# Opening in a hand-written order with squares summed on TensorE; hyperbolic tangents, split exponents and a filter emitted between the blocks

## The chip, the core and the metric

The kernel runs on one core of one Trainium2 chip. It is one launch that computes a whole inference step of a small four-stage network. The metric is the device time of the launch in microseconds (us), as the median of a few runs. The core has a matrix engine (PE, with its weight loads shown apart as PEld), a vector engine (DVE), a scalar engine with look-up functions (ACT), a general engine (POOL) and a queue processor that starts transfers (SP). Each engine works through its own list of instructions strictly in order and waits where the next one's inputs or buffers are not ready.

## The reference

Two groups of tokens, 128 context tokens and 512 latent tokens, run through one even and one odd layer at a width of 1024. The change touches only the first layer. Its first steps are an RMS norm over the width, an adaptive scale and shift made from the condition vectors, and one wide input projection:

```python
y = xf * lax.rsqrt(jnp.mean(xf * xf, axis=-1, keepdims=True) + EPS)    # norm, per token
h = y * (1 + scale) + shift             # scale, shift = linear map of silu(c)
proj = h @ P['ev_in_w'][e]
cv = _short_conv(proj[..., :EV_CONV], ...)
mq = jax.nn.silu(cv[..., o0:o0 + M_W])                 # mLSTM queries
mk = jax.nn.silu(cv[..., o0 + M_W:o0 + 2 * M_W])       # mLSTM keys
h = jax.nn.sigmoid(o) * h                              # mLSTM output gate
```

Beside the projection the kernel evaluates the long-convolution filter of the layer: a small network with sines on the positions (`_hyena_spectra`: features, sin, sin, a last linear map, an exponential window), normalised by the sum of magnitudes and transformed with a Fourier matrix. The mLSTM part then works in chunks, forwards and backwards, with exponents that are differences of running sums and maxima:

```python
dlog = jnp.where(mask, b[:, :, None] - b[:, None, :] + ic[:, None, :], -jnp.inf)
mt = jnp.maximum(b + m[:, None], jnp.max(dlog, axis=2))
w = jnp.exp(dlog - mt[:, :, None])          # weights within a chunk
a_in = jnp.exp(inter - mt)                  # weight of the state that comes in
```

## The kernel before, in words

Tokens (640 of them, 128 and 512) lie along the columns of a tile, the width along the partitions, so that x is eight tiles `x[0..7]` of 128x640. A matrix product that has to keep 32-bit accuracy is made of one-pass products of rounded operands: a tile is split into a high part (`hH`, `whi`, a rounding copy on ACT, L463 for weights and L1632 for activations) and a low part (`hL`, `wlo`, a subtraction on DVE or POOL, L464 and L1633). One step of a product is six matmuls, L1676 to L1681: high by high, low by high, high by low, each on 384 and on 256 columns. Eight such steps make an output tile of 128x640, called a block here. Data that is left as plain 32-bit floats goes through PE in slower matmuls, which the profile shows as two instructions each.

The first layer has these stages, in the order of the program.

- **Opening.** `mod_0` computes scale and shift (weights from `mod0`, 16 loads of 512 KB, matmuls at L1465, transposes at L1448). `norm_0` squares the eight x tiles on ACT (L1611), adds them up on DVE and POOL (seven additions, L1613, those in `RA` on POOL), lets PE sum over the partitions (five matmuls, L1551), takes the root on DVE (L1598 to L1603), spreads the result over the partitions (L1571 on DVE, L1575 on PE, L1580 on ACT), and multiplies x by it (L1619, the tiles in `XP` on POOL). Each tile is then scaled and shifted (L1629, L1631), rounded (L1632) and its low part is formed (L1633, those in `LP` on POOL). `sines` makes the inner network of the filter for three thirds of the positions (L509, L514, range reduction on DVE at L471 to L477). Only PE's order is written by hand here, by the string `START`, one letter for each step of the three generators (`m` modulation, `s` sines, `r` norm) and `g` for the first weights. The second eight loads of `mod0` each wait for a copy on POOL (L1440).
- **Blocks.** `mlstm_in` makes the gates' tile and the first convolution's tile (the two opening blocks), then seven more convolution blocks, the values (`values`, L807 to L810) and four gate blocks. `conv` (L639 to L648) is a three-tap convolution; the keys and queries go through Silu (L786, L787), the output gates through Sigmoid (L792) and a multiplication (L793). `mlstm_gates` does the running sums and maxima on DVE (L819 to L884).
- **Filter.** `filter` is emitted as a whole before `mlstm_in`: for two filters and two halves, three windows each (`windowed`, an exponential on ACT at L595, a product L602, magnitudes L604 and L606, sums L607, L610 and L611), a sum of magnitudes (`hy_norm`: L617 on DVE, L619 on PE, L622), and Fourier products (L557 to L559, L576 to L578).
- **mLSTM and the rest of the projection.** `mlstm` transposes the keys (L927), weights them (L940 on POOL), forms the states (L948 on PE, L950 and L952 on DVE) and then works through five chunks; its exponents come from 32-bit float matmuls (L990 and, for chunks 1 to 4, L1000) on right-hand sides that POOL and DVE prepare (`RH` at L979, L980 and L983). `hyena_in` makes the remaining blocks of the projection beside it.

Except for `START`, nothing sets the engines' orders by hand: the whole program runs under a list scheduler that simulates the engines while it takes the instructions in the order of emission, and it may put an instruction into another engine's idle time. A block's weights are loaded through a ring of tiles (`wraw`, four) and split into two pairs (`whi`, `wlo`). ACT holds one group of look-up functions at a time; changing the group costs an instruction of its own (ACT_TABLE_LOAD), and the list scheduler leaves them where the functions alternate.

## Time and profile before

| | us |
|---|---|
| median of 3 runs (2131.42 to 2133.31) | 2132.94 |
| the profiled execution | 2131.59 |
| its span | 2129.8 |
| PE busy in the span | 2005.5 (94%) |
| DVE busy | 1607.7 (75%) |
| ACT busy | 1099.9 (52%) |
| POOL busy | 740.3 (35%) |

The profiled execution took 1.79 us more than its span, and lies 1.35 us under the median. Times of the trace are counted from the start of the span. "Busy" of PE is the time with a matmul in flight; PE's clock is shown as the granted share of full speed, and everything that the change touches lies in the first 395 us, a fifth of the span.

### The profile page before, as it was taken

The page shows a single profiled execution, that of the slowest core. Times are in us where ns is not written, and L with a number is a line of the kernel's source. Part 1 is how long each engine was busy: PE and PEld are TensorE (multiplying, and loading weights), DVE is VectorE, ACT ScalarE, POOL GpSimd, SP SyncE. Part 2 cuts the span into 40 slices and gives each one's busy share as a digit, 9 for nine tenths or more (in the row PEclk, how much of TensorE's full clock was granted, in tenths as well). Part 3 has the DMA queues.
Part 4 walks back from the last instruction along what each step waited for, and adds up shares of the span by engine and source line. Part 5 has one row for each costly group of instructions (what it writes and reads, how often), then busy time and mean ns, then how long its engine had stood idle before and what let it go on. Part 6 is the DMA issues. An engine that isn't in the chain of part 4 may idle for free.

```text
span 2129.8 us, 35924 instructions
## 1 busy us (share of the span) xinstructions
PE 2005.5 (94%) x14034; PEld 1906.7 (90%) x14034; DVE 1607.7 (75%) x2685; ACT 1099.9 (52%) x1908; POOL 740.3 (35%) x751
## 2 busy tenths in 40 slices
PE   4999899998899999999899999999999899999997
PEld 2889788987899999999899899999999899999997
DVE  7875566787988888887687777776743988888885
ACT  3847634422655555555375556555522555555553
POOL 4411121343444443524232323333322343444422
PEclk9999999999899999999999999999999899999998
DMA  7654422764122222233222222121445122222221
GB/s 289 223 171 147 135 74 69 270 213 166 40 87 72 90 70 89 75 98 124 74 61 60 65 65 66 60 65 60 149 159 177 31 92 77 87 78 84 73 96 50
DMA packets 85637, 225.38 MB, mean 106 GB/s; under 512 B 9979, under 2 KB 27899, under 8 KB 85468
## 3 DMA queue, kind: packets, MB, share of 16 engines
q1 hardware_dynamic: 71756, 205.44, 29.4%
q10 hardware_dynamic: 8960, 9.86, 1.5%
q0 software_dynamic: 4752, 7.79, 1.4%
q8 instruction: 110, 1.80, 0.3%
q14 instruction: 59, 0.48, 0.1%
HBM read 204.86 MB, written 18.36 MB: 105 GB/s over the span
## 4 chain that ended last, share of the span: by engine, by line
PE 66%; DVE 14%; issue 2%; ACT 2%; DMA 2%; POOL 1%; SPq 0%; DVEq 0%; ACTq 0%; POOLq 0%
PE aux L2046 14%; PE mm L2046 14%; PE mm L1676 5%; PE mm L1680 5%; PE mm L1678 5%; PE mm L1677 3%; PE mm L1681 2%; PE mm L1679 2%; DVE x L1980 2%; PE aux L1321 1%; PE aux L1363 1%; PE aux L1342 1%; DVE sw L2012 1%; DVE wlof L2026 1%; PE md L1309 1%
## 5 line engine op out<-in xcount | busy, mean ns | idle before, releaser
L1680 PE MATMUL mm<-hH,wlo 128*128 128x384 f32 x760 | 264.0, 348 | 2.5 <-DVE wlo L464 2.5
L1676 PE MATMUL mm<-hH,whi 128*128 128x384 f32 x760 | 265.2, 349 | 1.2 <-ACT hH L1632 1.2
L1678 PE MATMUL mm<-hL,whi 128*128 128x384 f32 x760 | 263.5, 347 | 0.1
L463 ACT ACTIVATE whi<-wraw 128x1024 fp32r<-128x1024 f32 x108 | 114.1, 1056 | 205.7 <-PE mm L1679 109.3
L1677 PE MATMUL mm<-hH,whi 128*128 128x258 f32 (+1 forms) x568 | 168.9, 297 | 7.6 <-DVE U L641 7.4
L1679 PE MATMUL mm<-hL,whi 128*128 128x258 f32 (+1 forms) x568 | 167.3, 295 | 0.0
L1681 PE MATMUL mm<-hH,wlo 128*128 128x258 f32 (+1 forms) x568 | 166.5, 293 | 0.0
L464 DVE TENSOR_TENSOR wlo<-wraw,whi 128x1024 fp32r<-128x1024 f32 x94 | 120.6, 1283 | 46.5 <-ACT whi L463 42.2
L1680 PEld LDWEIGHTS mm<-hH,wlo 128*128 128x128 f32 x760 | 144.3, 190 | 6.5 <-issue 2.8
L1676 PEld LDWEIGHTS mm<-hH,whi 128*128 128x128 f32 x760 | 144.6, 190 | 4.8 <-issue 2.3
L1678 PEld LDWEIGHTS mm<-hL,whi 128*128 128x128 f32 x760 | 144.5, 190 | 2.6 <-issue 1.6
L464 POOL TENSOR_TENSOR wloe<-wraw,whie 128x512 fp32r<-128x512 f32 (+1 forms) x68 | 82.2, 1209 | 171.4 <-ACT whie L463 167.6
L1677 PEld LDWEIGHTS mm<-hH,whi 128*128 128x128 f32 x568 | 109.7, 193 | 12.4 <-issue 10.9
L1679 PEld LDWEIGHTS mm<-hL,whi 128*128 128x128 f32 x568 | 109.7, 193 | 2.3 <-issue 1.5
L1681 PEld LDWEIGHTS mm<-hH,wlo 128*128 128x128 f32 x568 | 109.7, 193 | 1.2 <-issue 0.5
L2026 DVE TENSOR_TENSOR wg<-sw,wg 128x1024 fp32r<-128x1024 f32 (+1 forms) x68 | 76.8, 1129 | 24.4 <-ACT wg L2007 23.4
L2007 ACT ACTIVATE wg<-sw 128x1024 fp32r<-128x1024 f32 (+1 forms) x68 | 64.4, 947 | 58.5 <-DVE sw L2016 37.6
L1318 POOL TENSOR_TENSOR xw<-xB,ec 128x256 f32<-128x256 f32 x64 | 49.2, 772 | 125.6 <-PE aux L1321 77.6
L2026 DVE TENSOR_TENSOR wlo<-wraw,whi 128x1024 fp32r<-128x1024 f32 (+1 forms) x68 | 76.7, 1128 | 15.5 <-ACT whi L2007 15.5
L2007 ACT ACTIVATE whif<-sw 128x1024 fp32r<-128x1024 f32 (+1 forms) x68 | 64.5, 948 | 39.7 <-DVE sw L2016 34.5
L2026 DVE TENSOR_TENSOR wlof<-sw,whif 128x1024 fp32r<-128x1024 f32 (+1 forms) x68 | 76.5, 1125 | 5.9 <-ACT whif L2007 5.2
L2166 ACT ACTIVATE nt<-nt 128x128 f32<-128x128 f32 x44 | 17.8, 404 | 109.5 <-POOL nt L2151 106.8
(804 smaller groups left out, 7160.2 us busy)
## 6 DMA issues: line engine op xcount, KB each, us to landing
wraw<-in_w SPq DMA_DIRECT2D x96, 512.0 KB, 3.5
modr<-in_modw SPq DMA_DIRECT2D x80, 512.0 KB, 6.1
wraw<-in_odw SPq DMA_DIRECT2D x49, 512.0 KB, 3.6
wraw<-in_w2q SPq DMA_DIRECT2D x48, 384.0 KB, 3.1
wraw<-in_evw SPq DMA_DIRECT2D x25, 512.0 KB, 4.2
wraw<-in_odow SPq DMA_DIRECT2D x16, 512.0 KB, 3.5
kd<-kst ACTq DMA_DIRECT2D x16, 256.0 KB, 2.6
wraw<-in_evow SPq DMA_DIRECT2D x8, 512.0 KB, 6.9
```

The source lines that it names most:

```text
L463: self.nc.scalar.activation(h, src, AF.Copy)
L464: (eng or self.nc.vector).tensor_tensor(lo, src, h.bitcast(F32), op=ALU.subtract)
L1318: nc.gpsimd.tensor_tensor(xw, xB[c][:, 0:256].rearrange("p (h e) -> p h e", h=4), self.ec[:, c, hd[d]].unsqueeze(2).to_broadcast([128, 4, ...
L1676: nc.tensor.matmul(pA, h, rh[k][:, 0:384], start=f, stop=False)
L1677: nc.tensor.matmul(pB, h, rh[k][:, 384:T_], start=f, stop=False)
L1678: nc.tensor.matmul(pA, h, rl[k][:, 0:384], start=False, stop=False)
L1679: nc.tensor.matmul(pB, h, rl[k][:, 384:T_], start=False, stop=False)
L1680: nc.tensor.matmul(pA, lo, rh[k][:, 0:384], start=False, stop=l)
L1681: nc.tensor.matmul(pB, lo, rh[k][:, 384:T_], start=False, stop=l)
L2007: vec, sub, copy = nc.vector.tensor_tensor, ALU.subtract, lambda o, v: nc.scalar.activation(o, v, AF.Copy)
L2026: vec(lo, r1 if step == "LA" else self.v, h.bitcast(F32), op=sub)
L2046: self.k.nc.tensor.matmul(bank, w, x, start=first and k == j == 0, stop=k == self.K - 1 and j == 2, skip_group_check=not first)
```

## The change

1. `start` takes the place of `mod_0` and `norm_0`, and the order of all engines is written by hand up to the end of the first two output tiles, not only PE's. The squares are still taken on ACT, but each square tile goes to PE directly: five matmuls a tile with the square as the weights and a column of ones as the moving operand, all 40 adding into one column group. All products of x with the root and all low parts of the activations are on DVE. The sines step one third after the other (`sine_steps`). The second eight loads of `mod0` no longer wait for copies on POOL. The two opening blocks are made in the order steps 0 to 3 of the first, shift and scale matmuls, steps 0 to 3 of the second, then steps 4 to 7 of both.
2. The filter is a generator that is advanced once after each convolution block, each gate block and every second value tile, and finished after `mlstm_in`.
3. Silu becomes a hyperbolic tangent and a DVE operation, y(1 + tanh y) on halved convolution weights; Sigmoid becomes a tangent of half the argument and (1 + tanh) times a halved factor.
4. The mLSTM exponents are made by one one-pass matmul each (18 of them) whose operands carry high and low parts in separate partitions. `mlstm` prepares the left sides once (`UR`) and the right sides' rows (`MR`, `XR`); each of the 18 then takes one DVE product of 128x512 (L997 of the new file).
5. Loads that waited for the last modulation matrix or for nothing (`filter_loads`, `mlc`) wait for the last low tile of the activations.

The core of the diff (long parts are left out where a line holds only three dots):

```diff
-START = 'sssmmrmmmrmmmmmrgsssmmmmmmmmmmr'
...
-                    with tc.manual_schedule(engines={mybir.EngineType.PE}):
-                        for c in START:
...
+                    with tc.manual_schedule():
+                        get, pr, pk, h2 = self.start(vp, fp, a, b, sq)
+                    self.filter_loads(fp, self.hL[LM].bitcast(F32)[:, 0:1])
                     self.load_mats(matp, self.hL[LM].bitcast(F32)[:, 0:1])
-                    f = self.filter(fp, h2)
-                    for _ in f:
-                        pass
+                    self.filt = self.filter(fp, h2)
                     self.bg.append(self.mod(0, (2, 3, 4, 5), fp, 4, self.mu[:, 0:1]))
...
-                    self.mlstm_in(vp, get)
+                    self.mlstm_in(vp, get, pr, pk)
                     self.mid = False
+                    for _ in self.filt:
+                        pass
...
-            nc.scalar.activation(o[:, 0:128], y[:, 0:128], AF.Silu)
-            nc.scalar.activation(o[:, 128:640], y[:, 129:641], AF.Silu)
+            for s, e, q in ((0, 128, 0), (128, 640, 1)):
+                nc.scalar.activation(o[:, s:e], y[:, s + q:e + q], AF.Tanh)
+                nc.vector.scalar_tensor_tensor(o[:, s:e], o[:, s:e], 1.0, y[:, s + q:e + q],
+                                               op0=ALU.add, op1=ALU.mult)
+            next(self.filt, None)
...
-                nc.scalar.activation(y[:, s:e], pr[g], AF.Sigmoid)
-            nc.vector.tensor_scalar(y[:, 0:T], y[:, 0:T], self.mng[:, h:h + 1], None, op0=ALU.mult)
+                nc.scalar.activation(y[:, s:e], pr[g], AF.Tanh, scale=0.5)
+            nc.vector.tensor_scalar(y[:, 0:T], y[:, 0:T], 1.0, self.mng[:, h:h + 1], op0=ALU.add, op1=ALU.mult)
...
+        fr = self.t(p, (128, T), "xm")
+        nc.vector.tensor_tensor(fr[64:128].rearrange("p (c s) -> p c s", s=128),
+                                MN[64:128].rearrange("p (c s) -> p c s", s=128),
+                                MP[64:128].unsqueeze(2).to_broadcast([64, 5, 128]), op=ALU.add)
+        UR, MR, XR = [], [], []
+        for d in range(2):
...
+            nc.scalar.activation(t, UL[d], AF.Copy)
+            nc.vector.tensor_tensor(t[other], UL[d][own], t[own].bitcast(F32), op=ALU.subtract)
+            nc.vector.tensor_copy(t[other2], UL[d][own2])
+            UR.append(t)
+            for src, lst, one in ((MN, MR, 1.0), (fr, XR, 0.0)):
+                t = self.t(p, (128, T), f"MX{d}{int(one)}", 1, F32R)
+                nc.gpsimd.memset(t[0:64].bitcast(F32), one)
+                nc.scalar.activation(t[own2], src[own2], AF.Copy)
+                nc.vector.tensor_tensor(t[other2], src[own2], t[own2].bitcast(F32), op=ALU.subtract)
+                lst.append(t)
...
-            nc.gpsimd.tensor_copy(RH[0:64], dl[0:64])
-            nc.vector.tensor_tensor(RH[64:128], mn, dl[64:128], op=ALU.mult)
-            if c:
-                RH2 = self.t(p, (128, 4, 128), "RH2", 2)[64:128]
-                stt(RH2, mn, MP[64:128, c:c + 1], dl[64:128], op0=ALU.add, op1=ALU.mult)
+            def exponents(src, d):
+                t = self.t(p, (128, 4, 128), "RH", 3, F32R)
+                nc.vector.tensor_tensor(t, src[d].bitcast(F32)[:, cs].unsqueeze(1).to_broadcast([128, 4, 128]), dl,
+                                        op=ALU.mult)
+                g = self.ps("aux")
+                nc.tensor.matmul(g, UR[d][:, cs], t.rearrange("p h t -> p (h t)"), start=True, stop=src is XR)
+                return g
...
+        def square(d):
             nc.scalar.activation(sq[d], self.x[d], AF.Square)
-        for i, (a, b) in enumerate(((0, 1), (2, 3), (4, 5), (0, 2), (6, 7), (4, 6), (0, 4))):
-            (nc.gpsimd if i in RA else nc.vector).tensor_tensor(sq[a], sq[a], sq[b], op=ALU.add)
+            for c in range(5):
+                nc.tensor.matmul(pc[:, c:c + 1], sq[d][:, 128 * c:128 * c + 128], self.ones[:, 0:1],
+                                 start=False, stop=d == 7 and c == 4)
...
+        product(0, range(4))
+        mods(1, 1, range(4))
+        ev = evac(1)
+        step(0)
+        turn(1, 1, ev)
+        product(1, range(4))
+        mods(1, 0, range(4))
...
+        for i in range(2):
+            product(i, range(4, 8))
```

The new order shows in the engines' lists. PE's list begins as follows in the program before; L1465 are the modulation's matmuls, L1551 the sum of the squares, L1575 the spreading of the root.

```order
1 L509 MATMUL aux<-q_88 64x512 x3
2 L1465 MATMUL mm<-wraw,scond 32x128 x8
3 L1465 MATMUL mm<-whi,scond 32x128 x8
4 L1551 MATMUL mm<-ones,k_188 128x1 x5
5 L1465 MATMUL mm<-wlo,scond 32x128 x8
```

In the changed program the sum of the squares is L1624, the modulation's matmuls L1596, the spreading L1661.

```order
1 L1619 MATMUL md<-rst,ones 128x5
2 L498 MATMUL aux<-q_88 64x512 x3
3 L1624 MATMUL md<-ones,k_115 128x1 x20
4 L1624 MATMUL md<-ones,stage 128x1 x10
5 L1624 MATMUL md<-ones,q_88 128x1 x5
6 L1624 MATMUL md<-ones,gates 128x1 x5
7 L1596 MATMUL aux<-wraw,scond 32x128 x8
8 L1596 MATMUL aux<-whi,scond 32x128 x8
9 L1596 MATMUL aux<-wlo,scond 32x128 x8
10 L1596 MATMUL aux<-wraw,scond 32x128 x8
11 L1661 MATMUL mm<-gates,ones 128x128 x5
```

The sum's matmuls moved ahead of every modulation matmul and became 40 instead of 5.

Second, the place on PE between the last of the four gate blocks and the transposes of the keys. Before, after the last step of the block (L1681) stand two magnitude sums of the filter, the six Fourier products of one short window, and then the transposes (L927):

```order
1213 L1681 MATMUL mm<-hH_507,wlo 128x256
1214 L619 MATMUL aux<-ones,kacc 128x1 x2
1215 L576 MATMUL aux<-kb,fwdc 128x256
1216 L577 MATMUL aux<-kb,fwdc 128x256
1217 L578 MATMUL aux<-kb,fwdc 128x256
1218 L576 MATMUL aux<-kb,fwdc 128x256
1221 L927 MATMUL aux<-cst,k_1323 128x128 x20
```

In the changed program the same place (last step L1796) is followed by modulation matmuls (L1466), the magnitude sums (L610) and the first of 48 Fourier products of a long window (L547 to L549); the short window and the transposes come after those.

```order
1159 L1796 MATMUL mm<-hH_370,wlo 128x256
1160 L1466 MATMUL md<-modr,scond 32x256 x16
1161 L1477 MATMUL md<-cst,modev 128x128 x2
1162 L610 MATMUL aux<-ones,kacc 128x1 x2
1163 L547 MATMUL aux<-kb,fwd 128x256
1164 L548 MATMUL aux<-kb,fwd 128x256
1165 L549 MATMUL aux<-kb,fwd 128x256
```

The last half of the filter, Fourier products included, moved behind the last block. Third, DVE's list between the filter's last split and the first state (`Cx`). Before:

```order
265 L464 TENSOR_TENSOR kb<-kb 128x512
266 L919 CAST idb<-cst 128x128
267 L980 TENSOR_TENSOR RH<-rb,dl 64x512 x2
268 L983 SCALAR_TENSOR_TENSOR RH_2984<-rb,MP,dl 64x512
269 L983 SCALAR_TENSOR_TENSOR RH_3059<-rb,MP,dl 64x512
270 L952 COPY Cx<-aux 128x129 x2
```

After, where L997 are the products for the exponents and L919 to L935 the new preparation:

```order
287 L449 TENSOR_TENSOR kb<-kb 128x512
289 L919 TENSOR_TENSOR xm<-rb,MP 64x640
290 L928 TENSOR_TENSOR UR_2825<-UL_720,UR_2825 32x640
291 L929 CAST UR_2825<-UL_720 32x640
292 L935 TENSOR_TENSOR MX_2829<-rb,MX_2829 32x640
293 L928 TENSOR_TENSOR UR_2837<-gates,UR_2837 32x640
295 L935 TENSOR_TENSOR MX_2841<-rb,MX_2841 32x640
296 L997 TENSOR_TENSOR RH<-MX_2829,dl 128x512
298 L935 TENSOR_TENSOR MX_2833<-xm,MX_2833 32x640
301 L969 COPY Cx<-aux 128x129 x2
```

Four operations ahead of the first state became twelve; POOL's eight weightings of the keys (L940 before, L957 after) stand in POOL's list at the same place in both programs.

## Rows read from the trace of the kernel before

**Rows 1.** The engines' busy time by stage: bounds of the stretch in us, its length, then busy us and instructions of PE, PEld, DVE, ACT and POOL, the granted share of PE's clock, the share of the transfer engines and GB/s. The stretches are the blocks up to the first magnitude sum of the filter, up to the second, up to the last gate block, the way to the transposes of the keys, and the mLSTM stage.

```profile
72.00:104.80 32.80, 30.88 (x253) 28.28 (x251) 30.58 (x32) 27.42 (x46) 12.58 (x13) 1.00 0.76 255
104.80:130.40 25.60, 21.77 (x184) 20.53 (x185) 23.63 (x58) 12.38 (x24) 0.64 (x1) 0.91 0.43 144
130.40:253.40 123.00, 119.36 (x956) 110.96 (x957) 71.91 (x95) 82.64 (x139) 25.20 (x25) 0.98 0.46 156
253.40:263.30 9.90, 3.06 (x13) 2.46 (x12) 6.35 (x12) 5.64 (x9) 0.00 (x0) 0.78 0.28 97
281.00:395.00 114.00, 114.00 (x738) 100.17 (x738) 70.94 (x180) 47.56 (x110) 15.15 (x15) 0.99 0.28 89
```

**Rows 2.** The order in time on PE in the opening: start us, us, what ran, how many, and in brackets how long PE stood idle before it and what ended that.

```profile
4.44 5.38 PE L509 MATMUL aux<-q 33*64 33x512 f32 x6 [4.44 <-DMA q<-in_hya]
...
23.98 2.29 PE L1551 MATMUL mm<-ones,k 128*128 128x1 f32 x10 [6.54 <-DVE k L1613]
...
48.03 0.48 PE L1448 MATMUL mm<-cst,modev 128*128 128x128 f32 x1 [9.53 <-ACT modev L1473]
...
54.27 0.67 PE L1676 MATMUL mm<-hH,whi 128*128 128x384 f32 x1
72.08 0.28 PE L1681 MATMUL mm<-hH,wlo 128*128 128x256 f32 x1
```

**Rows 3.** The order in time on ACT (the first and the last square) and on DVE (the last addition of squares, the sum's arrival, the products of x with the root).

```profile
7.55 0.74 ACT L1611 ACTIVATE k<-hL 128x640 f32<-128x640 f32 x1 [4.23 <-DMA hL<-in_x]
...
20.20 0.72 ACT L1611 ACTIVATE gates<-hL 128x640 f32<-128x640 f32 x1
...
23.10 0.83 DVE L1613 TENSOR_TENSOR k<-k,stage 128x640 f32<-128x640 f32 x1
26.31 0.16 DVE L1557 COPY rstv<-mm 128x5 f32<-128x5 f32 x1 [2.39 <-PE mm L1551]
...
31.57 7.10 DVE L1619 TENSOR_TENSOR hL<-hL,rb 128x640 f32<-128x640 f32 x4
```

**Rows 4.** PE's weight loads for a matmul with one moving column at L1551, in the opening and at a later place in the program: shortest, median and longest in ns, first and last start.

```profile
L1551 PEld LDWEIGHTS mm<-ones,k x10: 288/333/333, 24.0 to 25.9; 128*128 128x128 f32 x10
...
L1551 PEld LDWEIGHTS md<-ones,sacc x10: 188/192/192, 1547.5 to 1548.5; 128*128 128x128 f32 x10
```

**Rows 5.** The granted clock and the engines' work in short stretches, columns as in rows 1.

```profile
55.00:57.50 2.50, 2.50 (x11) 2.50 (x11) 1.92 (x7) 1.29 (x3) 2.50 (x3) 0.50 0.20 55
57.50:60.00 2.50, 2.50 (x19) 2.50 (x18) 1.42 (x6) 2.45 (x5) 1.16 (x4) 1.00 0.98 301
...
260.00:264.00 4.00, 3.46 (x14) 3.12 (x15) 1.40 (x5) 1.07 (x2) 0.00 (x0) 0.50 0.33 131
```

**Rows 6.** The order in time on DVE between the opening and the second magnitude sum: the first and the last row of the stretch of 45.6 us up to the end of the first magnitude sum, and the first and the last row of the gates' scans and constants.

```profile
59.19 0.68 DVE L522 TENSOR_TENSOR h2l<-win,h 64x512 fp32r<-64x512 f32 x1
...
103.94 0.83 DVE L617 TENSOR_TENSOR kacc<-kacc 128x256 f32<-128x256 f32 x1
...
106.02 0.82 DVE L826 SCALAR_TENSOR_TENSOR q<-q 64x640 f32<-64x640 f32 x1
...
124.52 0.87 DVE L884 TENSOR_TENSOR ends<-ends 64x4 f32<-64x4 f32 x10
```

**Rows 7.** PE's waits between 60 and 300 us: for whom, us in total, times, longest.

```profile
PE aux L619 <- DVE kacc L617: 13.8, 5, 6.6
```

**Rows 8.** ACT's loads of look-up tables between 60 and 262 us, grouped by the line that needs them: how many, us in total, mean ns.

```profile
L595 ACT ACT_TABLE_LOAD x11 | 14.1, 1283 | 0.1
...
L786 ACT ACT_TABLE_LOAD x7 | 9.0, 1283 | 0.1
...
L792 ACT ACT_TABLE_LOAD x4 | 5.1, 1283 | 0.1
```

**Rows 9.** The order in time on PE around the last gate block: three of its last matmuls, the magnitude sum, the transposes of the keys.

```profile
253.13 0.28 PE L1679 MATMUL mm<-hL,whi 128*128 128x256 f32 x1
253.25 0.34 PE L1680 MATMUL mm<-hH,wlo 128*128 128x384 f32 x1
253.42 0.28 PE L1681 MATMUL mm<-hH,wlo 128*128 128x256 f32 x1
260.26 0.98 PE L619 MATMUL aux<-ones,kacc 64*128 64x1 f32 x4 [6.56 <-DVE kacc L617]
...
263.32 3.52 PE L927 MATMUL aux<-cst,k 128*128 128x128 f32 x20
```

**Rows 10.** The order in time on DVE, POOL and PE between the transposes and the mLSTM stage, and the same DVE operation later, alone.

```profile
270.19 7.10 DVE L983 SCALAR_TENSOR_TENSOR RH<-rb,MP,dl 64x512 f32<-64x512 f32 x2
...
266.24 3.49 POOL L940 TENSOR_TENSOR r<-kS,wa 128x512 f32<-128x512 f32 x3 [15.06 <-ACT kS L929]
...
271.27 5.47 POOL L940 TENSOR_TENSOR r<-kS,wa 128x512 f32<-128x512 f32 x5
...
277.67 1.23 PE L948 MATMUL aux<-v,r 128*128 128x129 f32 x4 [4.67 <-DVE Cx L952]
...
319.69 0.75 DVE L983 SCALAR_TENSOR_TENSOR RH<-rb,MP,dl 64x512 f32<-64x512 f32 x1
```

**Rows 11.** The order in time on PE for one exponent in 32-bit floats, a pair of instructions, and what comes behind it.

```profile
303.40 1.02 PE L990 MATMUL aux<-RH,gates 128*128 128x512 f32 x2
304.26 0.38 PE L991 MATMUL aux<-mkb,idb 128*128 128x512 bf16 x1
```

277 lines of the change are left out of this document (172 added, 105 removed).

## The prediction

> **What bounds the kernel now.** I read the stage table first, then PE's waits, then the order in time on PE, ACT, DVE and POOL in the stretches that the diff touches. Everything touched lies before 395 us. In the opening PE is fed late: it stands idle 6.54 us for the added squares and 9.53 us for a modulation copy, and its first product of an output tile starts at 54.27, the last of the two opening blocks at 72.08 [rows 2]. From 72 to 130 DVE is the fullest engine, 30.6 of 32.8 us and 23.6 of 25.6, while PE has gaps [rows 1]; the gaps are waits for the filter's magnitude sums, 13.8 us in five places, with the longest of 6.6 [rows 7, 9]. From 130 to 253 PE is busy 119.4 of 123.0 us, and in the mLSTM stage from 281 to 395 without a gap, 114.0 of 114.0, while DVE has 43 us to spare there [rows 1]. So an earlier opening is worth something only where DVE then keeps up, a DVE operation saved or added counts before 130, and a PE instruction saved counts in the mLSTM stage.
>
> **Squares, root, first blocks.** The additions leave DVE and POOL and become 40 matmuls, two instructions each. Ten such instructions started over 1.9 us in the opening, where weight loads took 333 ns, and over 1.0 us late in the program at 192 ns [rows 4]: 0.21 and 0.11 us an instruction, so 80 take 16.9 or 8.9 us. They can start when the sines' three matmuls end, at 4.44 + 5.38 = 9.8 [rows 2], and the squares come at 0.74 us from 7.55 on [rows 3]: eight, with one operation of the sines between them, are done at about 14.2 instead of 20.9. The sum is then there at 18.7 or 26.7; I take 20.5, nearer the fast row since PE works without a gap, against 26.3 before [rows 3]. Root and spreading cost the same 5.2 us. The eight products with x, which took DVE 7.1 us for four beside POOL [rows 3], take some 0.82 each alone (the price of the last addition, 0.83), 6.6 us in all. The first product of a block should start near 35. But its steps 2 and 3 need the second pair of split weights, and steps 4 to 7 the second half of scale and shift, which are emitted between; with 6 us of DVE and ACT work behind those I get the end of both blocks at 65.5 (62 to 74), against 72.2: 6.7 us earlier.
>
> **What DVE makes of it.** Before, DVE runs from 59.19 to the end of the first magnitude sum at 104.77, 45.6 us [rows 6]. In the changed order the last low part ends near 59.5, and these things differ up to the first magnitude sum: low parts and scaling already done -2.4; waits that the earlier inputs fill -5.0; the gates' scans and constants now ahead of it, +14.7 (106.02 to 125.39 [rows 6], 19.4 without 3.8 of other work in it and 0.9 that stays behind); constants that stood in the opening +2.5; three tangent products of two pieces +2.7; one weight split +1.2; one convolution +1.8; the third sine's reduction and small operations +2.9. The sum is 64.0, so the first magnitude sum is ready near 123. PE has then done 13 us more block work than at its first sum before (104.8), and before reaches that position at about 121, with the half clock after its stalls. The opening's gain is gone, by DVE. From the second sum on PE has enough work again; I take 0 for opening and early blocks, with ends of -3 and the full +6.7.
>
> **Tables.** Tanh and the exponential share a group here, if the 22 table loads of this stretch go: 14.1 + 9.0 + 5.1 = 28 us of ACT [rows 8]. ACT is busy 82.6 of 123 us there [rows 1] and was waited for by PE hardly at all, so I count nothing for them by themselves; the cover is DVE and PE. Their share in the stalls is in the next term.
>
> **Filter between the blocks, and the tail.** Up to the last gate block PE loses the smaller stalls (1.7 + 0.9 of the 13.8) and 48 Fourier products with some sums, 6.6 us, that now stand behind it; with the half clock after stalls I get 253.4 - 13 = 240 (236 to 244) for the end of that block. What follows it is longer. Before: 6.6 us for the short window's chain, 3.1 us for its products, transposes at 263.3 [rows 9]. Now the long window's chain comes first, of about the same 6.6 us; then POOL's four sums, the split and 48 products of 256 columns, at 0.12 us full clock (253.13 to 253.25 [rows 9]) or twice that at the half clock granted after such a stall [rows 5], 5.8 to 11.5, I take 8; then the short window's chain, which can overlap those, and its 3.1: 24 us (17 to 30), transposes near 264. Net 0, between -5 and +4.
>
> **Transition to the mLSTM stage.** Before, PE stands idle 4.67 us for the first state copy, queued on DVE behind two L983 operations that took 7.10 us together while one alone takes 0.75 [rows 10]; POOL was weighting keys meanwhile (3.49 + 5.47 = 9.0 us) [rows 10]. In the changed list twelve preparations and products stand there, about 8.8 us alone (seven with two inputs of 640 columns at up to 0.82, three products at 0.7, two copies at 0.5), behind them the same state copy, and PE behind that, once the banks for states are full. PE's list has 34 block matmuls ahead of the first state's matmuls and more between these, some 16 us in all by my count until a bank must be free. So the stall goes, with 2 us of half clock, if DVE is done within that. By the rows the lock adds up to 2.9 us to an operation met by a POOL one; all of POOL's 9.0 us would make 17.8. I take +4, between -9 and +6.
>
> The Trainium skill, SBUF — State Buffer, section Who interferes with whom, says that a DVE instruction with two SBUF inputs contends with a GpSimd instruction that reads SBUF and that the one issued second is blocked for the whole of the other. That speaks against this part: by it each product could wait for a whole weighting, the 17.8 us end; the L983 rows agree with it, and if it held for all of them the term would be near -2 instead of +4.
>
> **Exponents in the mLSTM stage.** 18 exponents took 36 instructions. A pair occupies PE from 303.40 to 304.26, 0.86 us [rows 11], so 15.5 us. A one-pass matmul goes at 0.29 us for 640 columns (253.13 to 253.42 [rows 9]), 0.23 for 512: 18 take 4.2. PE has no gap there, so 11.3 us is the upper end. DVE gains some 6 us (18 products of 0.69 against 9), with 43 free; a product that arrives late may cost PE a gap, so I take +10, from 4.
>
> Sum: 0 + 0 + 4 + 10 = 14 us. From the profiled execution's 2131.59 this is 2117.6; that lies 1.35 under the median of the runs, so I predict 2118.5.
>
> **Rivals.** A: the opening's gain survives and the tail is short. The list of DVE is full, which speaks against it, but the waits of 5 us could be larger after the change of tables. Then 6.7 + 4 + 4 + 10 = 25, some more with a better transition: about 2106. B: DVE becomes the bound at the exponents, since each of the 18 needs its product just before; 43 us of free time speak against it, PE's in-order queue for it. Half of PE's saving goes, and 2 us of the transition: 2126. C, slower: at the transition the lock between DVE and POOL holds all products up, 9 us lost instead of 4 won, and PE has no block left to do; and with the longer tail (-6) this takes more than the exponents' 10 us. It decides from the point where the DVE chain ahead of the first state copy exceeds 16 us. The rows of the L983 pair speak for it, the free blocks against: 2138. D, the change doesn't do what it says in the opening: PE runs its 40 sums at the half clock, the sum is there at 26.7, no earlier than before, and everything behind it about 8 us later than forecast: 14 - 8, 2126.5.
>
> **Chances.** Forecast 0.45 (alone 2113 to 2125), A 0.17, B 0.18, C 0.12, D 0.08. Eight times in ten this gives 2104 to 2135. A change of this kernel can be told from none at about 0.2%, 4.3 us, so faster means under 2128.7: 0.41 + 0.17 + 0.13 + 0.06 = 0.77; the same, up to 2137.2: 0.04 + 0.05 + 0.02 + 0.02 = 0.13; slower 0.10, out of C.
>
> **What would show it.** The sum's arrival on DVE near 20.5 and the last step of the opening blocks near 65; the first magnitude sum on PE between 118 and 126 with DVE nearly full from 60 on; no table load between 80 and 250; the last gate block's end near 240 and the transposes' start near 264, with two waits of PE on magnitude sums between them; twelve DVE operations before the first state copy, their durations telling whether they met POOL; PE without a gap in the mLSTM stage and 18 exponent matmuls of some 0.23 us pitch. I am wrong if the transposes start before 258 or after 270, if PE waits for a product of the exponents for more than 5 us in all, or if the stages behind 395 us shift against each other.

## The result and the profile after

| | before | changed |
|---|---|---|
| median, us | 2132.46 | 2156.79 |
| ratio of the runs, 95% interval | | 1.0104 (1.009 to 1.0117) |
| the profiled execution, its span | 2131.59, 2129.8 | 2151.48, 2149.3 |
| mean granted clock of PE | 0.971 | 0.96 |

By the ratio the change costs 1.04%, some 22 us, where a gain of 14 was forecast. The changed kernel ran 2151.48, 2155.61 and 2157.97 us, and once 4656.62, a disturbed run that the median holds and the ratio leaves out. The profiled execution is the first of these, so stretches of its trace add up to a little less loss than the medians show. In the stage table of the changed kernel (columns as in [rows 1]) the first stretch is the opening up to the end of the first two output tiles, the second the blocks up to the end of the last gate block, the third the way to the transposes of the keys, the fourth the mLSTM stage.

```profile
0.00:76.60 76.60, 60.89 (x492) 48.49 (x492) 39.34 (x87) 28.73 (x47) 11.39 (x33) 0.89 0.71 255
76.60:252.60 176.00, 163.44 (x1269) 154.20 (x1269) 131.61 (x212) 97.21 (x186) 31.22 (x30) 0.94 0.48 168
252.60:278.90 26.30, 15.28 (x107) 13.10 (x106) 14.28 (x23) 10.61 (x20) 5.64 (x7) 0.73 0.21 73
281.00:395.00 114.00, 109.92 (x784) 106.76 (x782) 87.69 (x198) 53.85 (x123) 25.61 (x18) 0.98 0.30 93
```

The opening ends at 76.6 us, 4.4 later than before [rows 2]. The blocks take 176.0 us where before the way from 72.2 to 253.5 took 181.3. The tail takes 26.3 us instead of 9.8 [rows 9], at a granted clock of 0.73. So the transposes start at 278.9 instead of 263.3: 4.4 - 5.3 + 16.5 = 15.6 us late. The opening's PE is busy 60.9 us here; that share says nothing of when the blocks begin.

The same place by place, in starts on PE read from the traces of the two kernels (outputs: the last transpose of the mLSTM output; inverse: the last inverse transform; next: the first product of the next sub-layer):

| us | first magnitude sum | keys | first chunk | outputs | inverse | next | span |
|---|---|---|---|---|---|---|---|
| before | 104.8 | 263.3 | 298.3 | 389.8 | 527.5 | 575.0 | 2129.8 |
| changed | 137.0 | 278.9 | 315.8 | 400.0 | 536.1 | 594.2 | 2149.3 |
| difference | 32.2 | 15.6 | 17.5 | 10.2 | 8.6 | 19.2 | 19.5 |

The loss has two parts: up to the keys, and between the last inverse transform and the next sub-layer, where nothing was edited. Between the two the exponents give some 7 us back.

The order in time on PE in the opening, changed kernel, against [rows 2]: the features' products, the sum of the squares, the spreading of the root, and the first of the output tiles' matmuls behind each wait.

```profile
6.03 5.38 PE L498 MATMUL aux<-q 33*64 33x512 f32 x6
11.34 8.69 PE L1624 MATMUL md<-ones,k 128*128 128x1 f32 x40
19.89 4.41 PE L1624 MATMUL md<-ones,stage 128*128 128x1 f32 x20
24.16 2.27 PE L1624 MATMUL md<-ones,q 128*128 128x1 f32 x10
26.29 2.27 PE L1624 MATMUL md<-ones,gates 128*128 128x1 f32 x10
...
32.06 1.65 PE L1661 MATMUL mm<-gates,ones 128*128 128x128 f32 x10
...
42.57 0.64 PE L1721 MATMUL mm<-hH,whi 128*128 128x384 f32 x2 [3.36 <-ACT hH L1692]
...
50.00 0.90 PE L1721 MATMUL mm<-hL,whi 128*128 128x384 f32 x2 [2.45 <-DVE hL L1696]
```

The 80 instructions of the sum run from 11.34 to 28.5 without a gap: 17.2 us, 0.215 each. Their weight loads, against [rows 4], all but the first take 333 ns:

```profile
L1624 PEld LDWEIGHTS md<-ones,k x40: 286/333/333, 11.3 to 19.6; 128*128 128x128 f32 x40
...
L1624 PEld LDWEIGHTS md<-ones,gates x10: 333/333/333, 26.2 to 28.1; 128*128 128x128 f32 x10
```

On DVE, against [rows 3] and [rows 6], the sum arrives at 28.60, later than the 26.31 of before. The products with x begin at 34.17 (31.57 before), the last low parts at 67.00, and the gates' constants wait 4.95 us for a small load (`mlc`).

```profile
28.60 0.17 DVE L1648 COPY rstv<-md 128x5 f32<-128x5 f32 x1 [11.64 <-PE md L1624]
34.17 1.56 DVE L1672 TENSOR_TENSOR hL<-hL,rb 128x640 f32<-128x640 f32 x2
67.00 1.56 DVE L1696 TENSOR_TENSOR hL<-stage,hH 128x640 fp32r<-128x640 f32 x2 [0.47 <-ACT hH L1692]
78.23 0.15 DVE L861 COPY MP<-mlc 32x1 f32<-32x1 f32 x1 [4.95 <-DMA mlc<-in_mlc]
```

Around the last gate block, against [rows 9], PE's order in time shows the tail: the last step of the block, two magnitude sums 16 us apart with a wait before each, then the transposes.

```profile
252.47 0.28 PE L1796 MATMUL mm<-hH,wlo 128*128 128x256 f32 x1
259.67 1.01 PE L610 MATMUL aux<-ones,kacc 128*128 128x1 f32 x4 [3.64 <-DVE kacc L608]
275.83 0.98 PE L610 MATMUL aux<-ones,kacc 64*128 64x1 f32 x4 [6.10 <-DVE kacc L608]
278.89 2.33 PE L944 MATMUL aux<-cst,k 128*128 128x128 f32 x10
```

PE's waits between 60 and 300 us, against [rows 7], hardly changed for the sums, 12.9 us after 13.8; only their place did. The second row is the wait for the first state copy, 4.67 us before [rows 10].

```profile
PE aux L610 <- DVE kacc L608: 12.9, 3, 6.1
...
PE aux L965 <- DVE Cx L969: 2.9, 1, 2.9
```

The table loads of [rows 8] are gone; of 22 none is left, and one (for L839) is new:

```profile
L839 ACT ACT_TABLE_LOAD x1 | 1.3, 1283 | 0.0
```

Before the first state, against [rows 10]: two rows of the exponents' products and the state copy on DVE, the weightings on POOL.

```profile
286.90 2.87 DVE L997 TENSOR_TENSOR RH<-MX,dl 128x512 fp32r<-128x512 f32 x2
...
294.40 0.49 DVE L969 COPY Cx<-aux 128x129 f32<-128x129 f32 x2
```

```profile
284.85 12.45 POOL L957 TENSOR_TENSOR r<-kS,wa 128x512 f32<-128x512 f32 x8 [1.52 <-ACT kS L946]
```

A product takes 1.43 us here and 0.69 in the median of all 18. POOL's eight take 12.45 us in place of 9.0. The state copy comes 16.65 us after the first preparation (277.75), yet PE waits 2.87 us for it, less than the 4.67 of before, since it has blocks to do.

One exponent in the mLSTM stage, against [rows 11], is one instruction, and the next starts 0.24 us later.

```profile
320.21 0.40 PE L1000 MATMUL aux<-RH,UR 128*128 128x512 f32 x1
320.45 0.39 PE L1008 MATMUL aux<-mkb,idb 128*128 128x512 bf16 x1
```

Last, the part of the program that nobody edited: PE's order in time behind the inverse transforms, where the modulation of the next sub-layer (L1466) waits for its weights.

```profile
538.40 1.07 PE L1466 MATMUL md<-modr,scond 128*32 128x256 f32 x16 [2.07 <-DMA modr<-in_modw]
544.76 1.94 PE L1466 MATMUL md<-modr,scond 128*32 128x256 f32 x16 [5.29 <-DMA modr<-in_modw]
```

After the second wait the granted clock of 541 to 551 is 0.51 on the mean, and PE is busy 5.73 of these 10 us. Before had no wait for these weights between its last inverse transforms and 580 us.

### The profile page after: what moved, and what is told of

It reads as the page before. It is cut to its first block, busy times and chain, and to the rows that moved or that the text cites. A ratio compares the mean times of both kernels' runs of the same rounds, so it can differ in the third digit from the quotient of the medians.

```text
span 2149.3 us, 36008 instructions
## 1 busy us (share of the span) xinstructions
PE 2020.5 (94%) x14088; PEld 1931.7 (90%) x14088; DVE 1618.4 (75%) x2727; ACT 1074.5 (50%) x1892; POOL 710.8 (33%) x732
## 4 chain that ended last, share of the span: by engine, by line
PE 73%; DVE 18%; ACT 3%; issue 3%; DMA 3%; POOL 1%; ACTq 0%; DVEq 0%; SPq 0%; POOLq 0%
PE aux L2161 14%; PE mm L2161 14%; PE mm L1791 5%; PE mm L1793 5%; PE mm L1795 5%; PE mm L1792 3%; PE mm L1794 3%; PE mm L1796 3%; DVE x L2095 2%; PE aux L1336 1%; PE aux L1378 1%; PE md L1466 1%; PE aux L1357 1%; DVE sw L2127 1%; DVE wlof L2141 1%
## 5 line engine op out<-in xcount | busy, mean ns | idle before, releaser
L1795 PE MATMUL mm<-hH,wlo 128*128 128x384 f32 x744 | 259.5, 349 | 4.3 <-DVE wlo L449 4.3
L1791 PE MATMUL mm<-hH,whi 128*128 128x384 f32 x744 | 260.6, 351 | 0.0
L1793 PE MATMUL mm<-hL,whi 128*128 128x384 f32 x744 | 258.9, 348 | 0.0
L1792 PE MATMUL mm<-hH,whi 128*128 128x258 f32 (+1 forms) x552 | 163.9, 297 | 7.4 <-DVE U L632 7.2
L1794 PE MATMUL mm<-hL,whi 128*128 128x258 f32 (+1 forms) x552 | 161.8, 293 | 0.0
L1796 PE MATMUL mm<-hH,wlo 128*128 128x258 f32 (+1 forms) x552 | 161.8, 293 | 0.0
L1795 PEld LDWEIGHTS mm<-hH,wlo 128*128 128x128 f32 x744 | 141.8, 191 | 6.3 <-DVE wlo L449 5.1
L1791 PEld LDWEIGHTS mm<-hH,whi 128*128 128x128 f32 x744 | 142.2, 191 | 3.0 <-issue 2.4
L1793 PEld LDWEIGHTS mm<-hL,whi 128*128 128x128 f32 x744 | 142.1, 191 | 2.0 <-issue 1.3
L1792 PEld LDWEIGHTS mm<-hH,whi 128*128 128x128 f32 x552 | 106.4, 193 | 9.8 <-issue 7.7
L1794 PEld LDWEIGHTS mm<-hL,whi 128*128 128x128 f32 x552 | 106.2, 192 | 1.0 <-issue 0.2
L1796 PEld LDWEIGHTS mm<-hH,wlo 128*128 128x128 f32 x552 | 106.0, 192 | 0.9 <-issue 0.2
```

The lines of the kernel that those rows point to most:

```text
L1791: nc.tensor.matmul(pA, h, rh[k][:, 0:384], start=f, stop=False)
L1792: nc.tensor.matmul(pB, h, rh[k][:, 384:T_], start=f, stop=False)
L1793: nc.tensor.matmul(pA, h, rl[k][:, 0:384], start=False, stop=False)
L1794: nc.tensor.matmul(pB, h, rl[k][:, 384:T_], start=False, stop=False)
L1795: nc.tensor.matmul(pA, lo, rh[k][:, 0:384], start=False, stop=l)
L1796: nc.tensor.matmul(pB, lo, rh[k][:, 384:T_], start=False, stop=l)
```

## The experiments

All ratios are to the program before, timed on the same chip, with 95% intervals. A diff that undoes a part of the change is shown against the changed kernel.

### Each part alone

`only_opening`, `only_filter`, `only_tanh` and `only_exponents` are the program before with one part of the change (the opening with the filter's loads of part 5). The edits are those of the diff above, so only the switch of the filter is shown, as every kernel without part 2 has it:

```diff
                     self.filt = self.filter(fp, h2)
+                    for _ in self.filt:
+                        pass
```

> The kernel before with the new opening alone (old filter emission, Silu and Sigmoid, 32-bit exponents; the small constant tile of the gates is loaded without a gate). Theory 1 (the opening is what costs: the sum of squares is ready on PE only at 28 us, the two opening blocks end near 76 instead of 72, and DVE then starts its full stretch late): 12 to 17 us slower than before, about 2147, first magnitude sum on PE 10 us or more later than before's 104.8. Theory 2 (the filter between the blocks costs, the opening is neutral): within 4 us of before. Theory 3 (the tangent's operations on DVE cost): within 4 us of before.

> The kernel before with only the filter emitted between the blocks. Theory 2 (the filter's new place costs, by the chain that now stands behind the last gate block): 10 to 16 us slower, with the transposes of the keys 10 us or more behind before's 263.3. Theory 1 (the opening): within 4 us of before, the transposes within 4 us of 263.3. Theory 3: the same as theory 1.

> The kernel before with only the hyperbolic tangents in place of Silu and Sigmoid: 22 table loads go, 16 DVE products come. Theory 3 (DVE is the bound up to 130 us, so 2.7 us of products there and 8 in all push the magnitude sums): 4 to 8 us slower. Theories 1 and 2: within 4 us of before; a gain of up to 4 would say that the table loads had been on the path.

> The kernel before with only the split exponents. All theories on the early part: nothing changes before the transposes (263.3). My count for the mLSTM stage: 8 to 11 us gained there, 0 to 4 lost or won at the transition, 2121 to 2126 in all, unless the order of a later stage moves. Rival, the exponents give nothing because DVE becomes late: within 4 us of before.

| | median, us | ratio | keys | first chunk | outputs |
|---|---|---|---|---|---|
| only_opening | 2166.52 | 1.0164 (1.0147 to 1.0181) | 294.4 | 328.6 | 421.5 |
| only_filter | 2138.61 | 1.0029 (1.0018 to 1.004) | 272.5 | 306.7 | 400.3 |
| only_tanh | 2126.44 | 0.9972 (0.9963 to 0.9982) | 264.4 | 298.6 | 392.1 |
| only_exponents | 2125.49 | 0.9967 (0.9955 to 0.9979) | 263.5 | 300.0 | 383.9 |

Against 2132.11 us of the same chip: +34.4, +6.5, -5.7, -6.6. The sum is +28.6, a little more than all together cost. The opening is the part that costs, the two small parts gain. Of the sizes forecast only that of the exponents came true: the opening costs twice what theory 1 gave it, the filter's place less than theory 2 gave it, and the tangents gain where theory 3 had a loss. The exponents shorten the way from the first chunk to the outputs from 91.5 to 83.9 us, where forecast. For the tangents the gain is in the medians, but no stretch up to the outputs shows it in the one profiled execution, which at 2131.46 us was the slowest of ten.

### Why the opening is late

`sum_on_dve`: the squares are added on DVE and PE sums over the partitions alone, five matmuls.

```diff
-            for c in range(5):
-                nc.tensor.matmul(pc[:, c:c + 1], sq[d][:, 128 * c:128 * c + 128], self.ones[:, 0:1],
-                                 start=False, stop=d == 7 and c == 4)
...
+        for i, j in ((0, 1), (2, 3), (4, 5), (0, 2), (6, 7), (4, 6), (0, 4)):
+            nc.vector.tensor_tensor(sq[i], sq[i], sq[j], op=ALU.add)
```

> The changed kernel, but the squares are added on DVE (seven additions in the idle time that DVE had there) and PE sums over the partitions with five matmuls behind two units of the modulation, as before. Theory A (the 40 matmuls on PE at 0.21 us an instruction delay the sum, and this delay of the root reaches the first magnitude sum unshortened): the root's copy on DVE comes at 24 to 26 us instead of 28.6, the first magnitude sum on PE 3 to 5 us earlier than 137.0, the whole 3 to 6 us under the changed kernel's 2156.8. Theory B (the sum does not matter, the late filter weights and the gated constants do): magnitude sum and whole within 2 us of the changed kernel.

Measured 2141.31 us, 1.0036 (1.0022 to 1.005). The sum arrives 5.5 us earlier (23.06), but the first product of a block only 0.7 us (41.88), since PE ran the sines' and the modulation's matmuls behind the sum at half pace up to 38 us. The first magnitude sum comes at 139.8, 2.8 us later than in the changed kernel where theory A had it 3 to 5 earlier, and the keys at 283.1, 4.2 later. Of the place at the next sub-layer's first product it gains 9.8 us over the changed kernel (584.4 after 594.2), but the last inverse transform is at 537.0 after 536.1: what it wins lies behind that, not in the opening.

`early_loads`: the loads of part 5 wait for nothing, as in before.

```diff
-                    self.filter_loads(fp, self.hL[LM].bitcast(F32)[:, 0:1])
+                    self.filter_loads(fp, self.mu[:, 0:1])
...
-        nc.gpsimd.tensor_copy(c[:, 0:1], self.hL[LM].bitcast(F32)[:, 0:1])
```

> The changed kernel with the filter's loads released by the last modulation matrix instead of the last low tile, and the gates' small constant tile released by nothing, both as before. Theory B (the new gates make DVE wait 5 us for the constants and keep the filter's weights late): DVE's 4.95 us wait at 73 to 78 goes, the first magnitude sum comes 5 to 8 us earlier, the whole is 4 to 8 us under 2156.8. Theory A: the magnitude sum moves by less than 2 us, since DVE is full of other work.

Measured 2137.46, 1.0022 (1.0013 to 1.0032). The first magnitude sum comes 10 us earlier (127.0), as theory B has it, and the keys do not (279.8): the wait of 4.95 us for `mlc` is not on the path to the keys. The whole is 19 us under the changed kernel all the same, more than theory B's 4 to 8. In the profiled executions 7.2 us of that are there at the last inverse transform (528.9) and 16.8 at the next sub-layer's first product (577.4).

`no_filter_move` is the changed kernel with the whole filter emitted ahead of the blocks (the two lines shown above).

> The changed kernel with the filter emitted as a whole before the blocks, as before. If the parts add (the filter's new place costs 6.5 us alone): 2148 to 2152. If the new place helps where the filter starts late (the opening alone was 34 us slower, all four together 24): 2158 to 2168, with the transposes later than 278.9.

Measured 2141.09, 1.0042 (1.0025 to 1.0058); keys at 286.7, 7.8 us later than in the changed kernel. So with the late opening the filter between the blocks is no loss up to the keys. That the whole is nevertheless shorter, and shorter than either forecast, comes in the profiled execution (2146.14 us) again from behind the inverse transforms: the last of them is at 537.4, 1.3 us later than in the changed kernel, and the next product at 588.0, 6.2 earlier.

`early_sines` has the edit of `early_loads` and in addition brings the sines' steps forward (the first of them are shown); `early_sines_filter_first` has besides the filter ahead of the blocks.

```diff
             root(d)
         step(0)
+        step(0)
         ev = evac(0)
...
         scaled(3)
+        step(1)
         get(8)
+        step(0)
+        step(1)
         step(2)
```

> The changed kernel with the sines' second layer finished beside the first half of the low tiles, and the filter's and gates' loads released as before. Theory C (the filter is a chain of eight magnitude sums about 20 us apart whose start, 26 us late in the changed kernel, sets the transposes): first filter product on DVE near 66 to 75 instead of 97.5, first magnitude sum at 100 to 112, but with the last half of the filter still emitted behind the last block the transposes come at 268 to 274 (the place alone cost 9). Whole 2125 to 2135. Theory D (the start does not matter, early loads already brought the first sum 10 us forward and the transposes not at all): transposes at 277 to 281.

> The same with the filter emitted as a whole before the blocks, as before. Theory C: first magnitude sum at 98 to 110, transposes at 262 to 268, whole 2117 to 2128. Theory D: transposes past 276.

Measured 2132.72, 1.0004 (0.9995 to 1.0013), and 2136.79, 1.0018 (1.0008 to 1.0028). The first magnitude sum is at 111.5 and 111.3 us, 25 us earlier than in the changed kernel, and the keys at 273.7 and 278.8, only 5 and 0 us earlier. In the first kernel all three numbers lie in theory C's ranges; in the second the keys lie 11 us past C's range and in D's. So an earlier start of the filter moves the keys by a fifth of it or by nothing: it alone does not set them.

`wide_first` puts 24 wide matmuls on zeros at the head of PE's list; their result is not used.

```diff
+        wd = self.t(self.tp, (128, 256), "modev", 1)
+        nc.vector.memset(wd, 0.0)
+        wb, wp = wd.bitcast(BF16), self.ps("mm")
+        for _ in range(24):
+            nc.tensor.matmul(wp[:, 0:512], wb[:, 0:128], wb[:, 0:512], start=True, stop=True)
```

> The changed kernel with 24 matmuls of 128x512 in 16-bit floats on zeros (result unused) at the head of PE's list, ahead of the features' products and the sums of squares. Theory 'work': what PE does sets its pace; after 10 us of wide matmuls the 80 instructions of the sum run at about 0.11 us instead of 0.215, 8.6 to 10 us in all, and the sum reaches DVE at 26 to 31 us although it starts later. Rival 'time': PE is slow up to 31 to 36 us whatever it does; the 80 instructions still take over 15 us and the sum arrives at 36 to 40, and the whole is 4 to 10 us above the changed kernel.

One execution: 2159.06 us. PE's order in time, and its weight loads for the sum in two short windows (shortest, median, longest in ns; first and last start):

```profile
5.04 7.77 PE L1622 MATMUL mm<-modev 128*128 128x512 bf16 x24 [5.04 <-DVE modev L1619]
...
12.86 2.79 PE L498 MATMUL aux<-q 33*64 33x512 f32 x6
15.58 7.61 PE L1629 MATMUL md<-ones,k 128*128 128x1 f32 x40
23.05 4.41 PE L1629 MATMUL md<-ones,stage 128*128 128x1 f32 x20
```

```profile
L1629 PEld LDWEIGHTS md<-ones,k x6: 192/192/192, 16.0 to 16.6; 128*128 128x128 f32 x6
```

```profile
L1629 PEld LDWEIGHTS md<-ones,k x3: 325/333/338, 16.8 to 17.2; 128*128 128x128 f32 x3
```

The clock in this trace says the same (bounds in us, length, PE busy, granted clock, the share of the transfer engines, GB/s):

```profile
15.50:17.50 2.00, 2.00 (x15) 0.83 1.01 401
17.50:19.50 2.00, 2.00 (x11) 0.50 1.05 418
```

Neither theory held whole. The rival 'time' falls: behind the wide matmuls the features' products take 2.79 us instead of 5.38, so PE can be fast at 13 us. But the sum begins fast and drops to 333 ns at 16.8 with nothing right before it but its own one-column matmuls, and stays there; the 80 take 16.1 us and the sum arrives at 31.76. In this execution what PE had done before set its pace, and one-column matmuls, gapless as they are, were followed by the slow one.

`sum_one_pass` rounds the squares to 16-bit floats, so that the 40 matmuls are 40 instructions; the sum is a little less exact.

```diff
-            nc.scalar.activation(sq[d], self.x[d], AF.Square)
+            nc.scalar.activation(sq[d].bitcast(BF16)[:, 0:640], self.x[d], AF.Square)
...
-                nc.tensor.matmul(pc[:, c:c + 1], sq[d][:, 128 * c:128 * c + 128], self.ones[:, 0:1],
-                                 start=False, stop=d == 7 and c == 4)
+                nc.tensor.matmul(pc[:, 2 * c:2 * c + 2], sq[d].bitcast(BF16)[:, 128 * c:128 * c + 128],
+                                 on2, start=False, stop=d == 7 and c == 4)
```

> The changed kernel with the squares rounded to 16-bit floats, so that each of the 40 matmuls of the sum is one instruction instead of two (on two equal columns of ones); the sum is a little less exact. At 0.215 us an instruction it should end behind the last square, about 20.5 us, where the prediction had it. Theory 'sum': the late sum is what made the opening late; then root, first product (34 to 36 us, changed kernel 42.6), the end of both blocks (66 to 70, 76.6) and the first magnitude sum (127 to 130, 137) all come 7 to 9 us earlier and the whole is at 2145 to 2150. Rival 'pace': the time saved goes into modulation matmuls at the slow pace (0.85 us for sixteen's half instead of 0.44); first product not before 40, blocks end 74 to 77, the transposes of the keys within 3 us of 278.9.

Measured 2129.36, 0.9985 (0.9976 to 0.9995): 27 us less than the changed kernel. Theory 'sum' is borne out for the opening: the first product and the end of the blocks come earlier than its ranges, the first magnitude sum at the late end of its own. The whole lies 16 us below its range. The sum's arrival on DVE, then PE's order in time:

```profile
16.86 0.15 DVE L1652 COPY rstv<-md 128x5 f32<-128x5 f32 x1
```

```profile
15.18 0.29 PE L1628 MATMUL md<-on,gates 128*128 128x2 bf16 x5 [0.34 <-ACT gates L1626]
15.40 1.08 PE L1596 MATMUL aux<-wraw,scond 128*32 128x128 f32 x16
...
18.69 0.65 PE L1596 MATMUL aux<-wraw,scond 128*32 128x128 f32 x16 [0.20 <-DMA wraw<-in_mod]
...
30.69 0.90 PE L1725 MATMUL mm<-hH,whi 128*128 128x384 f32 x2 [3.88 <-ACT hH L1696]
...
63.35 0.45 PE L1725 MATMUL mm<-hH,wlo 128*128 128x384 f32 x2
68.75 0.55 PE L590 MATMUL aux<-hyw,h 128*128 128x256 f32 x1 [4.95 <-DVE hyw L482]
```

The sum waits for the squares now and not the reverse: five matmuls take 0.29 us, far less than the 0.215 an instruction that was expected. A group of sixteen modulation instructions takes 1.08 us at 15.40 and 0.65 at 18.69; the changed kernel has such a fast group only at 36.47, though its sines' products are fast from 33.76 (1.07 us, and 1.97 in `sum_on_dve`). That the full pace came earlier can't be put down to less one-column work alone: `sum_on_dve` has ten such instructions in place of 80, with waits of up to 5.15 us around them, and is slow longest of the three; its row:

```profile
36.66 1.07 PE L1596 MATMUL aux<-kb,scond 128*32 128x128 f32 x16
```

The first product is at 30.69 (42.57), the two blocks end at 63.8 (76.6), the first magnitude sum is at 130.0. The keys, at 272.1, gain 6.8 us of these 12.8. The gain grows behind them, in stages that were not edited: 7.6 us at the outputs, 13.8 at the last inverse transform and 23.6 at the next sub-layer's first product. So the sum's way through the keys is worth 7 us of the 27. Another 9.8 lie in the stretch that the next part is about; what gives 6.2 in the stage with the transforms is not shown.

`sum_one_pass_early_loads` has the edits of `sum_one_pass` and of `early_loads`, and `sum_one_pass_no_filter_move` those of `sum_one_pass` and `no_filter_move`.

> sum_one_pass with the loads of the filter's weights and of mlc waiting for nothing, as in early_loads: both terms of the opening that missed are taken away. Theory 'terms': with the sum early and the mlc wait gone (5.3 us in sum_one_pass) the opening is what the prediction reckoned; first magnitude sum at 120 to 126 (forecast 123), transposes of the keys at 263 to 268 (forecast 264), the whole at 2117 to 2124 us. Rival 'tail': as in early_loads, the first magnitude sum comes earlier but the filter's last sums do not; transposes at 270 to 273, the whole at 2126 to 2131.

> sum_one_pass with the whole filter emitted ahead of the blocks again, as the program before does. Theory 'placement': the filter's tail of 40 us behind the last block exists because each block releases one piece of the filter; emitted as a whole the scheduler fits it between, and with the opening early the transposes of the keys come at 255 to 266 and the whole at 2112 to 2124 us. Rival 'DVE': the filter and the gates share DVE, and emitted first the filter delays blocks instead, as in no_filter_move (7.8 us later than the changed kernel); transposes at 275 to 282, the whole at 2130 to 2138.

Measured 2133.80, 1.0012 (1.0003 to 1.0022), and 2127.57, 0.9984 (0.997 to 0.9998). Keys at 270.4 and 272.9, whatever the loads wait for and wherever the filter is emitted. Rival 'tail' holds for the keys of the first (the whole is 3 us above its range); of the second, placement fell, and DVE's range was missed by 2 us too. In all three kernels the last block ends at 232 to 235 us, and the tail is then 38 to 40 us. Three magnitude sums stand behind the last block there, and PE waits for them longer than in the changed kernel (`sum_one_pass`, 225 to 275 us):

```profile
PE aux L610 <- DVE kacc L608: 18.3, 3, 10.6
```

From the first to the last magnitude sum it takes 140 to 141 us in each, and 139.5 in the changed kernel, but 150 in `early_loads` and 160 in `early_sines`, where the first comes earlier; so this is no fixed pace. What sets the end is not shown; DVE is busy only 74.0 of the 120 us from 130 to 250 in the last kernel, so it isn't DVE's load alone.

### The late wait

`HT` is the number of pieces of the next sub-layer's modulation that are written into each step of the stage with the transforms; the list scheduler orders what is written.

```diff
-HT = 1
+HT = 2
```

`changed_two_ticks` is the changed kernel with it, `before_two_ticks` the program before, `tanh_exponents` the program before with parts 3 and 4, `tanh_exponents_ticks` the same kernel once more (one execution; the two kernels are equal line for line, so it is a repeat), `tanh_exponents_two_ticks` parts 3 and 4 with `HT` at 2.

> The kernel before with the tangents and the split exponents, without the new opening and with the filter emitted as before. If the two gains add (5.7 and 6.6 us alone): 2118 to 2122. If they share a cover: 2123 to 2127. If the order of a later stage moves against it: above 2127.

> The tangents and the exponents on the kernel before once more, one look. The wait of 6.9 us for a modulation matrix ahead of the next sub-layer is a matter of the order that the scheduler wrote, so it comes back: 6 to 8 us again, and the first product of the next sub-layer at 569 to 572.

> The changed kernel with two steps of the next sub-layer's modulation between the parts of the long convolution instead of one (one constant). If the 7.4 us that PE waits for the last modulation matrices at 536 to 547 come from too few of those steps being done earlier: that wait goes, the stretch from the last inverse transform to the next sub-layer's first product takes 47 to 50 us instead of 58, the whole is 6 to 10 us under 2156.8. If it comes from the early stage's delay: no change.

> Tangents and exponents without the opening and the filter, with two steps instead of one of the next sub-layer's modulation written between (HT = 2). Theory 'order': the 9 us that tanh_exponents lost behind the last inverse transform were an accident of the written order; the stretch from there to the next sub-layer's first product falls from 56.4 to at most 50 us and the whole to 2119 to 2124 us. Rival 'contention': the transfer of the weights is late by itself; the stretch stays over 54 and the whole at 2128 to 2131.

> The kernel before with HT = 2 alone, a control. Theory 'order': before has no such wait, so nothing is won: the stretch stays at 47 to 48 us and the whole within 4 us of 2132. Rival: two steps are better by themselves, then this is 8 to 13 us faster than before and the 13.6 us of changed_two_ticks say nothing on the late wait.

| | median, us | ratio | inverse | next | between |
|---|---|---|---|---|---|
| changed kernel | 2156.79 | 1.0104 (1.009 to 1.0117) | 536.1 | 594.2 | 58.1 |
| changed_two_ticks | 2143.18 | 1.0057 (1.0042 to 1.0072) | 536.1 | 583.8 | 47.7 |
| tanh_exponents | 2130.47 | 0.9992 (0.9981 to 1.0002) | 514.3 | 570.7 | 56.4 |
| tanh_exponents_ticks | 2128.66 | | 513.2 | 569.4 | 56.2 |
| tanh_exponents_two_ticks | 2121.58 | 0.9943 (0.9925 to 0.996) | 517.6 | 565.4 | 47.8 |
| before_two_ticks | 2131.45 | 0.9999 (0.999 to 1.0008) | 527.9 | 575.2 | 47.3 |

In the kernels with the wait (these and `wide_first`) the stretch takes 56 to 59 us, in all others of this document 47 to 51. Two pieces for one take it away in both kernels of the table that have it, and do nothing in the program before, which has not. Edits of the changed kernel's opening take it away too (`sum_one_pass`, 48.3), so a part of what they gain is this wait. Theory 'order' holds: some 10 us of the changed kernel's loss, and 9 of the small parts' gain, hung on the order in which the scheduler placed modulation that was not edited. The whole of `changed_two_ticks` falls by 13.6 us, more than the 6 to 10 expected. `tanh_exponents_two_ticks` is the fastest kernel here, 10 us under before by the medians and 12 by the ratio.

## Why the prediction was wrong

Its sum had four terms: 0 up to the keys, 4 at the transition, 10 for the exponents, none behind them. Read as gains from the table of places, they are -15.6, -1.9, +7.3 and -9.3, which makes -19.5 against +14.

**The opening, the step that failed first.** The sum was put at 20.5 us, "nearer the fast row since PE works without a gap". It came at 28.60: PE works without a gap and at 0.215 us an instruction, the slow row. This was rival D's mechanism, which had a chance of 0.08 and a price of 8 us. `wide_first` shows that the argument was wrong, since the gapless sum falls from the fast row to the slow one under way, and `sum_one_pass` that the step mattered: with the sum at 16.86 the blocks end at 63.8. From the sum's arrival to that end it was 45 us by forecast, 47 there and 48 in the changed kernel. So of the 11.1 us by which the opening ended too late (76.6 for 65.5), 8.1 are the sum's, 1.5 by its start at 11.34 instead of 9.8 and the rest by its pace, and 3 come behind it.

**DVE and the first magnitude sum.** Forecast 123, measured 137.0. Nine us of the 14 came in with the last low parts, which ended at 68.5 and not at 59.5, and 5 with a wait that was not counted, for `mlc`. The sum of DVE's work between came out right, 63.5 us for 64.0, but partly by luck: `early_loads`, without that wait, reaches the magnitude sum 56.6 us after its last low part. And the step that hung the early blocks on it was wrong: in `early_sines` the first magnitude sum comes 25 us earlier, and the keys only 5.

**Blocks and tail.** Blocks: 174.5 us forecast, 176.0 measured. Tail: 24 forecast, 26.3 measured, within the given 17 to 30. By places the net of 0 failed by the opening, 11.1 + 1.5 + 2.3 = 15. Yet the mechanism of the tail was only half right: it was reckoned from the last block, but where the opening ends as forecast, the last block ends at 232 and the keys still come at 270 to 273 and not at 264. More of the filter is then left behind the block, three magnitude sums with 18.3 us of waits; why those come no earlier stays open. So of the 15.6 us at the keys 6.8 are shown to be the sum's.

**Transition.** Forecast +4, measured -1.9, in its range. The twelve operations took 16.65 us, not the 8.8 alone, and the lock that was feared is there: products at twice their time beside POOL. A product takes 0.74 us more than in the median of all, and a weighting 0.5 more (1.55 in the median after 1.03 of before). The Trainium skill, SBUF — State Buffer, section Who interferes with whom, calls the ports that DVE and GpSimd (POOL) share an exclusive lock. The trace agrees in part: both sides pay, and neither for the whole of the other, since a weighting of before took 1.03 us and a product alone takes 0.69. The pair of L983 in before was misread as up to 2.9 us more for each: the first of the two took 4.9 us more than one alone and the second 0.7.

```profile
270.19 5.65 DVE L983 SCALAR_TENSOR_TENSOR RH<-rb,MP,dl 64x512 f32<-64x512 f32 x1
```

But PE waits only 2.87 us, as it has blocks to do; rival C's point of 16 us was reached and its price was not.

**Exponents.** Forecast +10 with an end at 4, measured +7.3 in the changed kernel and +7.6 alone. The instruction's price was right (0.24 us for 0.23). PE waits for no product of the exponents there, so B's mechanism did not show. A wait that the forecast didn't have stands at the end of the stretch: PE waits 5.6 us for the scaling of the last output on DVE (L983 of the new file, for the transposes at L988), 3.2 us in `only_exponents` and not at all in before.

```profile
PE aux L988 <- DVE kS L983: 5.6, 1, 5.6
```

**Tables.** They went, as forecast. Nothing was counted for them; alone the tangents gain 5.7 us by the medians.

**Behind 395 us.** Nothing was forecast; the text named a shift of these stages against each other as a case in which it would be wrong, without a price. It cost 9.3 us. The stretch between the last inverse transform and the next sub-layer is 10.6 us longer, and the experiments on `HT`, which take 10.4 of them back, show it to be the written order of modulation pieces.

So the sign came out as in rival C, with D's mechanism and a term that no case had.

## What to carry to other kernels

That PE works without a gap was no sign here that it works fast: price a sum of one-column matmuls by rows of the same form at the same place, not by whether PE is busy, and cut the number of its instructions first. In a program under a list scheduler, compare the places behind the edit in both traces before explaining a difference: here 10 us came from a stage that nobody had touched, and one constant put it right. A part that gains alone can hide that way too, so time parts alone and together.
